# Sums of the quarters of x for block pairs on GpSimd instead of VectorE

## The chip, the cores and the metric

The kernel runs on one core of a Trainium2 chip. The metric is the device time of one execution in microseconds. A core has a matrix engine (TensorE, PE in the profile), a vector engine (VectorE, DVE), an engine for activation functions (ScalarE, ACT), a general engine (GpSimd, POOL) and one that issues DMAs (SyncE, SP). Each works through its own queue in the order in which the kernel has issued its instructions, and waits at an instruction until what it needs from other engines is there.

## The reference

The kernel computes a small decoder of two layers for 256 tokens of width 1024, all in float32. Each layer has four parts, each between two RMS norms:

```python
x += 0.5 * post(SwiGLU_1(pre(x)))     # ffn(l, 0): (silu(x W_gate) * (x W_up)) W_out, width 2816
x += post(Mixer(pre(x)))              # layer 0: mLSTM; layer 1: differential attention
x += 0.5 * post(SwiGLU_2(pre(x)))     # ffn(l, 1)
x += post((p[i] W_ple) * sigmoid(pre(x) W_gate))
```

Between the layers, keys and values are computed once from the normed x. Nearly all the time goes into products of x (256 x 1024) with weight matrices that are read from HBM in blocks of 1 MB.

## The kernel before

**Float32 products out of three.** TensorE works on the type fp32r, which holds fewer bits than float32. So each operand is split in two: a high part (ScalarE copies it to fp32r: tiles `xh`, `whi`, `hh`) and the leftover (VectorE subtracts the high part: `xl`, `wlo`, `hl`). `split` does both. A product then takes three matmuls: high x high, low x high, high x low. A weight block of 1 MB is 128x2048 in SBUF (`wraw`), and its leftover is one VectorE operation on 128x2048; a quarter of x is 128x512.

**Block pairs.** The weights of a hidden layer come in blocks of columns, a block for each 256 columns. `block_pair` (from L718) computes two blocks for both halves of the tokens in seven products instead of eight, in the manner of Strassen and Winograd. For that it needs sums of weight blocks and sums of quarters of x. The weights are `w11`, `w21`, `w22` (blocks as they are), `wt3` and `wu1` (a block loaded by SyncE's DMA, with a second block added by an accumulating DMA that GpSimd issues) and `wt2`, `wt4` (VectorE adds two `wraw` tiles). The quarters are made in `forms` (L700 to L712), once for all the pairs of a part: with a11, a12, a21, a22 the quarters of the normed and transposed x (tiles `att`, 128x512 float32),

- s1 = a21 - a22
- s3 = a11 - a21
- s2 = s1 - a11
- n4 = a12 + s2

and each is split into `xh` and `xl`. `forms` is called five times: for ffn(0,0) (place 1), for the mLSTM's input product (place 2), for ffn(0,1) (place 3), ffn(1,0) (place 4) and ffn(1,1) (place 5). At places 3 to 5 its operations are marked urgent, since the pairs begin right behind the norm; at places 1 and 2 they are not. In the profile of the kernel before, the sums lie at 42.5 to 52.3, 213.9 to 226, 303.5 to 308, 514.6 to 518.4 and 797.5 to 803.7 us. All pairs of a part use the first product with w11 and w21 and the unsummed quarters; then s2 with wt2, s1 with wu1, s3 with wt3, n4 with w22.

**What sets the order.** The kernel's code isn't issued as it is written. A recording layer collects all operations with the tiles that they read and write; `cost` (L212 to L257) gives each a duration; `play` (L267 to L428) simulates the engines with these durations and gives every engine the order in which its operations are issued, urgent ones and those of higher rank first; and `issue` (L430) then issues them. So nearly every instruction of the profile has the line L433, and tiles tell them apart. The plan also hands out the buffers, so that a tile such as `wlo_4r` holds one thing in one plan and another thing in the next. `play` lets a GpSimd operation end no earlier than 170 ns after the last VectorE operation with two SBUF inputs; a VectorE operation waits in the plan for no GpSimd operation but those whose result it reads. A duration in `cost` that changes moves operations on every engine.

The other work of GpSimd is small: powers of the norms' means (tiles `sm`, 128x1), masks, and the accumulating DMAs of the pairs.

## Time and profile before

| what | value |
|---|---|
| median of three runs | 1003.71 us (1002.12, 1003.71, 1003.89) |
| the profiled execution's own time | 1002.59 us |
| its span in the trace | 1000.8 us |
| instructions in the trace | 12442 |
| granted TensorE clock | 0.997 |
| data read from HBM | 263.40 MB |
| GpSimd: busy time, instructions | 94.9 us, 126 |

The page gives for each engine the time in which it was busy, and its share of the span. A row of a timeline has the start in us, the duration, the engine, the line, the operation with its tiles (out<-in, buffer numbers of rotating tiles are part of the name where they matter), shapes and types, and the count where a row stands for several of the same kind; in brackets stand the idle time of the engine ahead of it and what ended that. A row of a group has the busy time in us and the mean of one in ns, then idle time. Engines' records overlap a little: a VectorE operation is shown until its result is written, and the next begins some 80 ns earlier.

### The profile page before, as it was taken

How to read it: one execution, taken by the hardware profiler on the slowest of the kernel's cores; microseconds unless marked ns; L12 is line 12 of the kernel's file. 1: busy time of each engine (PE TensorE's matmuls, PEld its weight loads, DVE VectorE, ACT ScalarE, POOL GpSimd, SP SyncE). 2: the span in 40 equal slices, each digit the busy share in tenths (PEclk: the TensorE clock that was granted, in tenths of full speed). 3: DMA queues.
4: the chain of work that ended last, by engine and by line, in shares of the span. 5: the costliest groups of instructions: out<-in, count | busy, mean ns of one | idle time of the engine just before them, and what ended most of it. 6: DMA issues, size and time to landing. Idle time of an engine off the chain costs nothing.

```text
span 1000.8 us, 12442 instructions
## 1 busy us (share of the span) xinstructions
PE 986.4 (99%) x4636; PEld 803.0 (80%) x4636; DVE 892.8 (89%) x909; ACT 698.6 (70%) x924; POOL 94.9 (9%) x126
## 2 busy tenths in 40 slices
PE   9999999999999999999999999999999999999997
PEld 7888888887787778888878888888888887878786
DVE  6977999799999999998799999898984999999983
ACT  7746777578756877685867767686776776757752
POOL 0010000300141000001120000001002300000010
PEclk9999999999999999999999999999999999999998
DMA  9999948765699999765699999864759899996621
GB/s 345 420 339 343 311 179 296 244 207 198 255 320 340 326 309 335 279 247 207 261 301 330 324 353 347 329 244 161 253 210 285 235 297 318 313 295 252 242 84 43
DMA packets 45859, 274.68 MB, mean 274 GB/s; under 512 B 5480, under 2 KB 5864, under 8 KB 16104
## 3 DMA queue, kind: packets, MB, share of 16 engines
q1 hardware_dynamic: 39752, 231.69, 60.2%
q0 software_dynamic: 5760, 41.95, 20.6%
q8 instruction: 36, 0.59, 0.2%
q10 hardware_dynamic: 288, 0.27, 0.1%
q14 instruction: 23, 0.19, 0.1%
HBM read 263.40 MB, written 10.49 MB: 274 GB/s over the span
## 4 chain that ended last, share of the span: by engine, by line
PE 47%; issue 2%; ACT 2%; POOL 1%; DVE 1%; DVEq 0%; POOLq 0%; ACTq 0%
PE accI L433 30%; PE accO L433 15%; PE tr L433 2%; POOL sm L433 1%; ACT sg L433 1%; DVE wlo_4r L433 0%; ACT att L433 0%; DVE wlo_2r L433 0%; ACT wraw L433 0%; ACT whi_5r L433 0%; ACT whi_0r L433 0%; DVE wraw L433 0%; DVE att L433 0%; DVE xl_5r L433 0%; DVEq L1498 0%
## 5 line engine op out<-in xcount | busy, mean ns | idle before, releaser
L433 DVE TENSOR_TENSOR wraw<-wraw,wraw 128x2048 f32<-128x2048 f32 x40 | 91.4, 2284 | 0.1
L433 ACT ACTIVATE whi_1r<-wraw 128x2048 fp32r<-128x2048 f32 (+2 forms) x49 | 72.7, 1494 | 18.2 <-PE accI L433 8.8
L433 ACT ACTIVATE whi_4r<-wraw 128x2048 fp32r<-128x2048 f32 (+1 forms) x45 | 75.4, 1684 | 11.9 <-issue 4.4
L433 ACT ACTIVATE whi_2r<-wraw 128x2048 fp32r<-128x2048 f32 (+1 forms) x48 | 79.4, 1661 | 5.5 <-issue 2.6
L433 ACT ACTIVATE whi_5r<-wraw 128x2048 fp32r<-128x2048 f32 (+1 forms) x47 | 79.2, 1694 | 5.6 <-PE accI L433 4.7
L433 ACT ACTIVATE whi_0r<-wraw 128x2048 fp32r<-128x2048 f32 (+2 forms) x48 | 74.5, 1557 | 6.8 <-PE accI L433 3.4
L433 ACT ACTIVATE whi_3r<-wraw 128x2048 fp32r<-128x2048 f32 (+1 forms) x45 | 73.6, 1647 | 3.3 <-PE accI L433 1.6
L433 ACT ACTIVATE att<-accI 128x512 f32<-128x512 f32 x80 | 47.5, 594 | 38.1 <-PE accI L433 37.8
L433 POOL DMA_DIRECT2D wraw<-in_ffn_in x36 | 32.0, 889 | 343.5 <-DMA wraw<-in_ffn_in 286.3
L433 POOL TENSOR_SCALAR sm<-sm 128x1 f32<-128x1 f32 x32 | 23.5, 735 | 308.8 <-ACT sg L433 308.8
L433 POOL TENSOR_TENSOR sm<-sm,mhalf 128x1 f32<-128x1 f32 (+2 forms) x40 | 30.7, 769 | 108.2 <-DVE sm L433 105.6
L433 ACT ACTIVATE sg<-att,sm 128x256 f32<-128x256 f32 x54 | 26.9, 502 | 16.9 <-DVE att L433 16.8
L433 ACT ACTIVATE sg<-accO 128x512 bf16<-128x512 f32 (+2 forms) x46 | 20.2, 445 | 25.0 <-PE accO L433 21.0
L433 ACT ACTIVATE sg<-accI,sm 128x256 f32<-128x256 f32 x34 | 16.0, 470 | 29.3 <-PE accI L433 27.3
L433 PEld LDWEIGHTS tr<-ident,sg 128*128 128x128 f32 x176 | 23.0, 140 | 14.6 <-DVE hl_2r L433 2.7
L433 PE MATMUL tr<-ident,sg 128*128 128x128 f32 x176 | 34.0, 274 | 0.3 <-DVE hl_2r L433 0.3
L433 DVE SCALAR_TENSOR_TENSOR wraw<-wraw,sm,wraw 128x512 f32<-128x512 f32 x32 | 22.7, 749 | 12.0 <-POOL sm L433 11.9
L433 DVE TENSOR_TENSOR att<-accI,att 128x512 f32<-128x512 f32 x40 | 27.4, 685 | 3.3 <-PE accI L433 2.9
L433 ACT ACTIVATE sg<-wraw 128x512 bf16<-128x512 f32 x32 | 20.1, 630 | 13.7 <-DVE wraw L433 9.7
L433 ACT ACTIVATE att<-accI,sm 128x512 f32<-128x512 f32 (+1 forms) x22 | 14.8, 671 | 20.8 <-PE accI L433 20.8
L433 DVE SCALAR_TENSOR_TENSOR sg<-att,sm,sg 128x256 f32<-128x256 f32 x54 | 25.7, 480 | 1.7 <-ACT sg L433 1.5
L433 DVE TENSOR_TENSOR att<-att,att 128x512 f32<-128x512 f32 (+1 forms) x33 | 22.4, 679 | 3.8 <-ACT att L433 3.6
(610 smaller groups left out, 3249.9 us busy)
## 6 DMA issues: line engine op xcount, KB each, us to landing
wraw<-in_ffn_in SPq DMA_DIRECT2D x102, 1024.0 KB, 9.4
wraw<-in_ffn_out SPq DMA_DIRECT2D x44, 1024.0 KB, 8.3
wraw<-in_ffn_in POOLq DMA_DIRECT2D x36, 1024.0 KB, 13.3
wraw<-in_mlstm_in SPq DMA_DIRECT2D x14, 1024.0 KB, 5.3
wraw<-in_ple_gate SPq DMA_DIRECT2D x8, 1024.0 KB, 5.1
wraw<-in_w_kv SPq DMA_DIRECT2D x8, 1024.0 KB, 4.8
home<-wraw SPq DMA_DIRECT2D x28, 256.0 KB, 5.1
wraw<-home SPq DMA_DIRECT2D x14, 512.0 KB, 5.4
```

The lines of the kernel that those rows point to most:

```text
L433: getattr(getattr(self.nc, eng), name)(*args, **kw)
```

## The change

The four sums in `forms` are issued to GpSimd instead of VectorE, and `cost` has a new rule for GpSimd's `tensor_tensor`: 560 ns for up to 8 elements a partition, 2.2 ns an element above (1126 ns for 512).

```diff
@@ cost, L256
         elif o.eng == "gpsimd":
-            o.dur = 560 if o.name == "tensor_tensor" else 320 + m
+            o.dur = 320 + m if o.name != "tensor_tensor" else 560 if m <= 8 else 2.2 * m
             o.lat = o.dur + 90
@@ forms, L709
         for out, x0, x1, op, q in (
                 (s1, a21, a22, ALU.subtract, q1), (s3, a11, a21, ALU.subtract, q3),
                 (s2, s1, a11, ALU.subtract, q2), (n4, a12, s2, ALU.add, q4)):
-            nc.vector.tensor_tensor(out, x0, x1, op=op)
+            nc.gpsimd.tensor_tensor(out, x0, x1, op=op)
             split(*q, out)
```

The order of all engines is as before up to place 1; from place 2 on the plan is a new one, with the same number of TensorE instructions.

Place 3, VectorE before. The rows begin with the leftovers of the quarters a11 and a22; `att_100`, `att_103`, `att_105` and `att_102` on the left are s1, s3, s2 and n4:

```order
L433 TENSOR_TENSOR xl_4r<-att_103,xh_4r 128x512
L433 TENSOR_TENSOR hl_0r<-tr_97,hh_0r 128x256
L433 TENSOR_TENSOR xl_0r<-att_99,xh_0r 128x512
L433 TENSOR_TENSOR att_100<-att_103,att_99 128x512
L433 TENSOR_TENSOR att_103<-att_105,att_103 128x512
L433 TENSOR_TENSOR att_105<-att_100,att_105 128x512
L433 TENSOR_TENSOR xl_2r<-att_100,xh_2r 128x512
L433 TENSOR_TENSOR xl_3r<-att_103,xh_3r 128x512
L433 TENSOR_TENSOR xl_1r<-att_105,xh_1r 128x512
L433 TENSOR_TENSOR att_102<-att_102,att_105 128x512
L433 TENSOR_TENSOR att_104<-accI_90,att_104 128x512
L433 TENSOR_TENSOR wraw_82<-wraw_82,wraw_85 128x2048
```

Three sums run in a row here, then their three leftovers, then n4; w21's leftover has been computed earlier.

Place 3, VectorE in the changed kernel; `att_98`, `att_105`, `att_103` and `att_100` are now s1, s3, s2 and n4, `wlo_4r` is the leftover of w21 and `wlo_2r` that of wt2:

```order
L433 TENSOR_TENSOR xl_4r<-att_105,xh_4r 128x512
L433 TENSOR_TENSOR xl_0r<-att_99,xh_0r 128x512
L433 TENSOR_TENSOR hl_0r<-tr_97,hh_0r 128x256
L433 TENSOR_TENSOR xl_2r<-att_98,xh_2r 128x512
L433 TENSOR_TENSOR xl_3r<-att_105,xh_3r 128x512
L433 TENSOR_TENSOR xl_1r<-att_103,xh_1r 128x512
L433 TENSOR_TENSOR wlo_4r<-wraw_79,whi_2r 128x2048
L433 TENSOR_TENSOR xl_4r<-att_100,xh_4r 128x512
L433 TENSOR_TENSOR wlo_2r<-wraw_82,whi_3r 128x2048
```

The sums are gone, and w21's leftover stands behind the leftovers of s1, s3 and s2.

Place 3, GpSimd in the changed kernel (`sm` are the norm's powers, the DMAs add a second block for the next pair):

```order
L433 TENSOR_SCALAR sm_0_156<-sm_15_149 128x1
L433 TENSOR_TENSOR sm_4_160<-sm_0_156,mhalf_133 128x1
L433 TENSOR_TENSOR att_98<-att_105,att_99 128x512
L433 TENSOR_TENSOR att_105<-att_103,att_105 128x512
L433 TENSOR_TENSOR att_103<-att_98,att_103 128x512
L433 TENSOR_TENSOR att_100<-att_100,att_103 128x512
L433 DMA wraw_77<-in_ffn_in 128x2048
L433 DMA wraw_83<-in_ffn_in 128x2048
```

Between the norm's power and the two DMAs, which followed it directly, four sums have come.

Place 4, VectorE in the changed kernel; `att_99`, the second `att_103` and `att_101` are s1, s3 and s2, `wlo_3r` is the leftover of the 128x2048 block w11 and `wlo_1r` that of w21, and the copies are of transposed tiles:

```order
L433 COPY wraw_81<-tr_97 128x4x128
L433 TENSOR_TENSOR xl_2r<-att_103,xh_2r 128x512
L433 TENSOR_TENSOR xl_4r<-att_102,xh_4r 128x512
L433 TENSOR_TENSOR xl_3r<-att_99,xh_3r 128x512
...
L433 COPY wraw_81<-tr_97 128x4x128
L433 TENSOR_TENSOR wlo_2r<-wraw_82,whi_5r 128x1024
L433 TENSOR_TENSOR xl_0r<-att_103,xh_0r 128x512
L433 TENSOR_TENSOR wlo_2r<-wraw_82,whi_5r 128x1024
L433 TENSOR_TENSOR wlo_3r<-wraw_83,whi_1r 128x2048
L433 TENSOR_TENSOR xl_5r<-att_101,xh_5r 128x512
L433 COPY wraw_81<-tr_97 128x4x128
```

The leftover of s3 comes behind four weight leftovers and a copy, that of s2 behind two more; before, the four sums stood between two of the copies.

Place 5, VectorE in the changed kernel; `att_98`, the second meaning of `att_105`, and `att_103` are s1, s3 and s2, and `wlo_4r` is the leftover of wt2:

```order
L433 TENSOR_TENSOR xl_6r<-att_105,xh_6r 128x512
L433 TENSOR_TENSOR xl_1r<-att_100,xh_1r 128x512
L433 TENSOR_TENSOR hl_0r<-tr_97,hh_0r 128x256
L433 TENSOR_TENSOR att_102<-accI_90,att_102 128x512
L433 TENSOR_TENSOR xl_5r<-att_98,xh_5r 128x512
L433 SCALAR_TENSOR_TENSOR sg_128<-att_102,sm_6_162,sg_128 128x256
L433 TENSOR_TENSOR xl_3r<-att_105,xh_3r 128x512
L433 TENSOR_TENSOR xl_2r<-att_103,xh_2r 128x512
L433 TENSOR_TENSOR hl_2r<-tr_97,hh_2r 128x256
L433 TENSOR_TENSOR wlo_4r<-wraw_76,whi_1r 128x2048
```

The rows are those of before without the sums; s1 stood ahead of `xl_6r`, the next two among the following leftovers.

## Prediction

> **What bounds the kernel now.** I read the page's busy shares first, then busy time by engine in the five stretches that hold the five places where the sums are computed (columns: from:to, length, then busy us and count for PE, PEld, DVE, ACT, POOL, then PEclk, DMA share, GB/s).

> ```profile
> PE 986.4 (99%) x4636; PEld 803.0 (80%) x4636; DVE 892.8 (89%) x909; ACT 698.6 (70%) x924; POOL 94.9 (9%) x126
> ...
> 40.00:100.00 60.00, 60.00 (x272) 49.43 (x271) 47.66 (x40) 35.09 (x36) 5.39 (x6) 1.00 1.02 354
> 186.00:250.00 64.00, 64.00 (x318) 52.10 (x317) 60.16 (x70) 48.09 (x59) 7.87 (x9) 1.00 0.63 206
> 300.00:360.00 60.00, 58.26 (x259) 45.51 (x258) 59.61 (x56) 45.19 (x52) 6.12 (x8) 1.00 1.00 330
> 490.00:540.00 50.00, 49.70 (x235) 40.44 (x234) 47.68 (x56) 36.30 (x52) 9.65 (x12) 1.00 0.89 292
> 780.00:850.00 70.00, 67.67 (x305) 54.44 (x304) 68.55 (x65) 51.79 (x60) 11.62 (x11) 1.00 0.90 283
> ```

> TensorE sets the time nearly everywhere: it is never idle in 40:100 and 186:250 and idle 0.30 us in 490:540. The page's 89% for VectorE hides two stretches in which VectorE is the bound: 59.61 of 60 us in 300:360, with TensorE idle 1.74, and 68.55 of 70 in 780:850, with TensorE idle 2.33. Two rows show that TensorE's waits there end on VectorE (the bracket is the idle time before the matmul, and what released it):

> ```profile
> 314.15 0.50 PE L433 MATMUL accI<-wlo_4r,xh_2r 128*128 128x512 f32 x1 [0.65 <-DVE wlo_4r L433]
> ...
> 832.76 0.50 PE L433 MATMUL accI<-wlo_2r,xh_5r 128*128 128x512 f32 x1 [1.03 <-DVE wlo_2r L433]
> ```

> So what GpSimd does is free (9% busy) unless it is late; what VectorE loses or gains counts at place 3 (ffn(0,1), 303 us) and place 5 (ffn(1,1), 797 us), with place 4 (ffn(1,0), 514 us) on the edge.

> **What is removed: 20 sums on VectorE.** At place 3 they stand so (DVE):

> ```profile
> 302.57 0.42 DVE L433 TENSOR_TENSOR hl_0r<-tr,hh_0r 128x256 fp32r<-128x256 f32 x1
> 302.90 0.68 DVE L433 TENSOR_TENSOR xl_0r<-att,xh_0r 128x512 fp32r<-128x512 f32 x1
> 303.50 2.14 DVE L433 TENSOR_TENSOR att<-att,att 128x512 f32<-128x512 f32 x3
> 305.60 0.69 DVE L433 TENSOR_TENSOR xl_2r<-att,xh_2r 128x512 fp32r<-128x512 f32 x1
> 306.20 0.68 DVE L433 TENSOR_TENSOR xl_3r<-att,xh_3r 128x512 fp32r<-128x512 f32 x1
> 306.81 0.69 DVE L433 TENSOR_TENSOR xl_1r<-att,xh_1r 128x512 fp32r<-128x512 f32 x1
> 307.41 0.68 DVE L433 TENSOR_TENSOR att<-att,att 128x512 f32<-128x512 f32 x1
> ```

> Each lasts 0.68 us, but the next starts 0.60 us after it (306.81 to 307.41): four sums are worth 4 x 0.60 = 2.4 us of VectorE per place, 12 us over five.

> **What is added: 20 sums on GpSimd.** No row of before has GpSimd adding 128x512. The nearest rows (GpSimd by form: busy, mean ns):

> ```profile
> L433 POOL MEMSET att<- 128x288 f32 x1 | 0.3, 341 | 27.9 <-DVE att L433 27.9
> L433 POOL MEMSET mhalf<- 128x8 f32 x1 | 0.1, 106 | 0.0
> L433 POOL MEMSET ident<- 128x128 f32 x1 | 0.2, 206 | 0.3 <-POOLq L1496 0.3
> L433 POOL TENSOR_SCALAR_AFFINE_SELECT ident<-ident 128x128 f32<-128x128 f32 x1 | 0.3, 287 | 0.0
> ```

> Writing costs (341-106)/280 = 0.84 ns an element; an operation that also reads one input costs (287-206)/128 = 0.63 ns more. If writing and two reads add up, a sum is 0.106 + 512 x 0.84 + 2 x 512 x 0.63 = 1.18 us, an estimate; if reads hide behind the write, 0.54; with a read as dear as a write, 1.40. I take 1.18, as the select row is the only one with an input. [...]

> One sum takes twice as long as on VectorE and the three of s1, s3, s2 are a chain on one engine. How the two engines get along is the next question:

> ```profile
> 293.97 4.20 POOL L433 TENSOR_SCALAR sm<-sm 128x1 f32<-128x1 f32 x1 [5.03 <-ACT sg L433]
> ...
> 301.12 0.30 POOL L433 TENSOR_SCALAR sm<-sm 128x1 f32<-128x1 f32 x1 [2.30 <-ACT sg L433]
> 301.51 0.56 POOL L433 TENSOR_TENSOR sm<-sm,mhalf 128x1 f32<-128x1 f32 x1
> ...
> 293.60 2.28 DVE L433 TENSOR_TENSOR wlo_2r<-wraw,whi_5r 128x2048 fp32r<-128x2048 f32 x1
> 295.80 2.28 DVE L433 TENSOR_TENSOR wlo_4r<-wraw,whi_2r 128x2048 fp32r<-128x2048 f32 x1
> ```

> The operation that takes 0.30 us at 301.12 takes 4.20 us at 293.97: it ends at 298.17, just behind two VectorE operations back to back (to 298.08) that read two SBUF tiles each. So a GpSimd operation waits for such VectorE operations, and doesn't get between two of them. Every leftover (xl, wlo) and every wraw sum is of that kind. Whether a long GpSimd operation holds VectorE in turn, no row shows.

> [...]

> **Places 1 and 2: 0.** Both are computed ahead of need; VectorE is busy 47.66 of 60 and 60.16 of 64 us there, and TensorE 60.00 of 60 and 64.00 of 64. If GpSimd held VectorE for all of 4 x 1.18, VectorE would lose 4.7 - 2.4 = 2.3 us, within 12.34 and 3.84 us of slack.

> **Place 3: +1.2 (0 to +1.9).** In the new order VectorE runs the leftovers xl_4r, xl_0r, hl_0r, then those of s1, s3 and s2, and only then w21's wlo_4r, which before stood ahead of the sums (295.80); it has changed places with a wraw sum (308.61 before) of the same 2.28 us, so the work behind is as much as it was. s1 can start beside hl_0r, which reads one SBUF tile; xl_4r, xl_0r before it end at 301.96 + 0.69 + 0.60 = 303.25. Without any holding: three sums, 303.25 + 3 x 1.18 = 306.8; ACT's high part, 0.62; the leftover of s2, 0.68: w21's turn at 308.1. Before, this point of the queue was reached at 308.01 (behind n4, which VectorE no longer computes): 0. With holding: s1 to 304.4, s3 to 305.6, leftover of s1 to 306.3, s2 to 307.5, leftover of s3 to 308.2, then either the leftover of s2 (w21 at 308.9) or n4 first (310.0): +0.8 to +1.9. ACT's part and the rows behind:

> ```profile
> 305.98 0.63 ACT L433 ACTIVATE xh_1r<-att 128x512 fp32r<-128x512 f32 x1
> ...
> 308.01 0.68 DVE L433 TENSOR_TENSOR att<-accI,att 128x512 f32<-128x512 f32 x1
> 319.47 2.28 DVE L433 TENSOR_TENSOR wlo_1r<-wraw,whi_4r 128x2048 fp32r<-128x2048 f32 x1
> 321.67 2.28 DVE L433 TENSOR_TENSOR wraw<-wraw,wraw 128x2048 f32<-128x2048 f32 x1
> ...
> 326.19 2.29 DVE L433 TENSOR_TENSOR wraw<-wraw,wraw 128x2048 f32<-128x2048 f32 x1
> ```

> Behind it VectorE runs without a gap until past 321.67, so the loss stays in its queue, and as VectorE is the bound TensorE pays it. I take +1.2, between the held cases and the free one, nearer to the held. The two accumulating DMAs of the next pair now stand behind four sums in GpSimd's queue (before: 302.11 and 304.01):

> ```profile
> 302.11 0.95 POOL L433 DMA_DIRECT2D wraw<-in_ffn_in  x1
> 304.01 0.86 POOL L433 DMA_DIRECT2D wraw<-in_ffn_in  x1 [0.94 <-DVE xl_0r L433]
> ...
> wraw<-in_ffn_in POOLq DMA_DIRECT2D x36, 1024.0 KB, 13.3
> ```

> Issued at about 309.4, the first lands at 322.7 (13.3 us), and its first reader is the wraw sum at 326.19: hidden by 3.5 us; a longer wait in GpSimd's queue than that would show.

> **Place 4: +1.2 (0 to +2.1).** The rows that count:

> ```profile
> 513.96 0.69 DVE L433 COPY wraw<-tr 128x512 f32<-128x512 f32 x1
> ...
> 520.16 0.69 DVE L433 COPY wraw<-tr 128x512 f32<-128x512 f32 x1
> ...
> 529.31 2.28 DVE L433 TENSOR_TENSOR wlo_3r<-wraw,whi_4r 128x2048 fp32r<-128x2048 f32 x1
> ...
> 532.82 0.47 PE L433 MATMUL accI<-wlo_3r,xh_1r 128*128 128x512 f32 x1
> ```

> The wlo_3r (w21) ends at 531.59 and is used at 532.82: 1.23 us of cover. If the engines take turns, s1 runs beside the copy, which reads no second SBUF tile, and three sums hold VectorE: 3 x 1.18 - 2.4 = +1.1, covered: 0. If GpSimd never gets between back-to-back operations, as at 293.97, s3 waits for the copy at 520.16 and s2 for a gap behind the next leftovers; by the order, w21's leftover then ends near 534.9 against 532.8: +2.1. The 4.20 us row is the only one on this question and shows starving, so I take a little more than the middle, +1.2.

> **Place 5: +1.0 (-0.4 to +1.2).**

> ```profile
> 797.46 0.69 DVE L433 TENSOR_TENSOR att<-att,att 128x512 f32<-128x512 f32 x1
> ...
> 804.59 2.28 DVE L433 TENSOR_TENSOR wlo_1r<-wraw,whi_2r 128x2048 fp32r<-128x2048 f32 x1
> ...
> 807.10 0.40 PE L433 MATMUL accI<-wlo_1r,xh_2r 128*128 128x512 f32 x1
> ```

> s1 starts at 797.46 before; in the new order two leftovers go first and s1 gets in beside hl_0r, at 798.8; s3 ends at 801.2, s2 at 803.1 (its turn comes behind the leftover of s1), the leftovers of s3 and s2 bring wt2's leftover to 805.8 to 806.0, against 804.59: +1.2 to +1.4. It ends at 806.87 and is used at 807.10, so 0.23 of it is covered: +1.0 to +1.2. Without holding it would start at 804.2, 0.4 earlier.

> **Sum.** 0 + 0 + 1.2 + 1.2 + 1.0 = +3.4 us; ends -0.4 and +5.2. The profiled execution took 1002.59 us (span 1000.8 and 1.8 around it), 1.1 below the median, 1003.71. On the median: 1003.71 + 3.4 = 1007.1; its own range is 1005 to 1009.

> **Rivals.**
> (A) GpSimd doesn't hold VectorE, and its chains end in time. For it: in before, GpSimd operations are so small that none is seen to delay VectorE. Against: the 4.20 us row shows that the two exclude each other. Sum of the lower ends: 0 + 0 - 0.4 = -0.4, so 1003.3.
> (B) The other side: the 2.4 us that VectorE is relieved of at places 3 and 5 comes through, and TensorE's waits in the stretches that VectorE bounds vanish; decisive is whether leftovers wait for sums or sums for leftovers. The cap is TensorE's idle time there, 1.74 + 2.33 = 4.1: 999.6. For it: 59.61 of 60 us busy. Against: s2's leftover needs three sums in a row, at 1.18 instead of 0.60.
> (C) Each sum holds VectorE for its whole 1.18 us at places 3 to 5: 3 x (4 x 1.18 - 2.4) = +7, and the changed order adds a wait of the size of the largest in before (1.03): 1011.7. For it: VectorE runs two-input operations back to back at all three. Against: part of each sum falls beside copies and PSUM reads.
> That the sums stay on VectorE is excluded: the order of the changed kernel has 20 additions of 128x512 on GpSimd.

> **How the numbers follow.** Forecast 0.45, A 0.25, B 0.15, C 0.15. Two times of this kernel differ by up to 0.18% (1002.12 to 1003.89), so 0.2%, 2 us, is what can be told from no change. Faster: B, and a little of A: 0.17. Same: most of A and the forecast's lower tail: 0.26. Slower: the rest of the forecast and C: 0.57. The range for 8 in 10 leaves out half of B and the tail of C: 1000.0 to 1012.5.

> **What would show it.** The 20 GpSimd rows: near 1.18 us where VectorE leaves gaps, 3 us and more where two-input operations run back to back. VectorE's next leftover should start when a sum ends, not inside it; if leftovers of 0.68 us overlap sums unchanged, rival A's step is right. At place 3 the matmul on w21's low part should wait for VectorE; in 300:360 TensorE's idle time should rise from 1.74 to about 3, in 780:850 from 2.33 to 3.3. Idle time below 1 in both, or a sum above 2 us in a gap of VectorE, would refute the forecast.

## The result, and the profile after

The changed kernel takes 1018.51 us (median of 4 runs, 1016.79 to 1019.40) against 1003.06 us before (median of 4): a ratio of 1.0154, 95% interval 1.0141 to 1.0168. It is slower by 15.5 us; the prediction had +3.4 and a range up to 1012.5.

The page's busy shares and busy time by stretch of the changed kernel (same columns as before; the stretches are later here by what has been lost ahead of them); its profiled execution took 1018.3 us with a span of 1016.4:

```profile
PE 992.6 (98%) x4636; PEld 806.5 (79%) x4636; DVE 898.3 (88%) x889; ACT 700.9 (69%) x924; POOL 128.6 (13%) x146
...
40.00:100.00 60.00, 57.61 (x253) 46.98 (x252) 43.95 (x35) 29.97 (x30) 5.73 (x7) 0.97 1.02 345
186.00:250.00 64.00, 62.16 (x305) 49.12 (x304) 56.98 (x61) 44.60 (x54) 14.19 (x16) 1.00 0.62 193
300.00:360.00 60.00, 56.31 (x242) 43.93 (x242) 57.67 (x47) 41.58 (x49) 15.50 (x12) 0.97 1.00 329
540.00:780.00 240.00, 237.63 (x1167) 194.16 (x1166) 217.19 (x228) 173.40 (x260) 16.21 (x23) 0.99 0.81 278
780.00:850.00 70.00, 68.15 (x326) 54.73 (x325) 59.18 (x62) 48.68 (x70) 19.23 (x19) 1.00 0.89 271
```

VectorE has 20 instructions less and is busy for 5.5 us more (898.3 against 892.8). TensorE, which was never idle in 40:100, is idle for 2.39 us there, and in two rows its granted clock is 0.97. Of these stretches only 780:850 has TensorE less idle than before.

Where the time goes is read best from TensorE's own progress. For the table, all its matmuls are added up by the columns that they stream, and it is noted how much later than in the trace of before the same sum is reached. The columns are points in the time of before: 56 lies behind place 1, place 2 between 205 and 290, place 3 between 290 and 370, place 4 between 500 and 560, place 5 between 790 and 960. The lower rows are runs of the next part. Each row is a single profiled execution: that of place 1 alone is the fastest of its five runs, that of place 2 alone the slowest of its five.

| later than before (us) at | 56 | 205 | 290 | 370 | 500 | 560 | 790 | 960 |
|---|---|---|---|---|---|---|---|---|
| changed kernel | 4.8 | 4.8 | 8.8 | 12.7 | 12.7 | 16.8 | 16.7 | 16.0 |
| new order, sums on VectorE | 1.7 | 1.8 | 5.6 | 6.5 | 6.5 | 8.8 | 8.7 | 7.1 |
| old order, sums on GpSimd | 1.2 | 1.2 | 2.7 | 5.1 | 5.1 | 5.7 | 5.5 | 6.0 |
| place 1 alone on GpSimd | 3.2 | 3.2 | 3.2 | 3.1 | 3.2 | 3.2 | 3.2 | 2.8 |
| place 2 alone | -0.2 | -0.2 | 3.9 | 3.7 | 3.7 | 3.6 | 3.5 | 4.5 |
| places 3 to 5 alone | -0.2 | -0.1 | -0.5 | 2.4 | 2.4 | 6.4 | 6.3 | 5.5 |

The loss comes in steps at places 1 to 4, about 4 us each, and place 5 loses nothing on balance.

At places 1, 3 and 4 a part of the step is a lower clock. In the changed kernel's trace, TensorE's granted clock is 0.50 in three stretches of 3.41 us each (from 46.74, 350.53 and 548.50), each of them behind waits of TensorE. By the ratio of the clocks, as an estimate, work that takes 3.41 us at 0.50 takes 1.7 at 1.00, so the three cost 5.1 us, a third of the loss. Between the first 7 and the last 6 us of the span, the traces of before, of both halves of the change (second and third row) and of place 1 alone have no such stretch; place 2 alone has one (from 835.93) and places 3 to 5 have two (from 312.69 and 537.97).

**What the sums do to VectorE.** Place 1, GpSimd and VectorE in the changed kernel:

```profile
30.21 1.30 POOL L433 TENSOR_TENSOR att<-wraw 128x512 f32<-128x512 f32 x1 [9.32 <-DMA wraw<-in_ffn_out]
31.58 3.21 POOL L433 TENSOR_TENSOR wraw<-wraw 128x512 f32<-128x512 f32 x1
34.87 3.23 POOL L433 TENSOR_TENSOR wraw<-att,wraw 128x512 f32<-128x512 f32 x1
38.18 2.16 POOL L433 TENSOR_TENSOR wraw<-wraw 128x512 f32<-128x512 f32 x1
...
30.37 3.28 DVE L433 TENSOR_TENSOR wlo_0r<-wraw,whi_5r 128x2048 fp32r<-128x2048 f32 x1
33.97 2.98 DVE L433 TENSOR_TENSOR wlo_1r<-wraw,whi_0r 128x2048 fp32r<-128x2048 f32 x1
37.20 4.22 DVE L433 TENSOR_TENSOR wlo_2r<-wraw,whi_1r 128x1024 fp32r<-128x1024 f32 x2
45.75 0.47 DVE L433 SCALAR_TENSOR_TENSOR sg<-accI,sm,sg 128x256 f32<-128x256 f32 x1
```

And VectorE in the same place before:

```profile
30.31 2.28 DVE L433 TENSOR_TENSOR wlo_0r<-wraw,whi_5r 128x2048 fp32r<-128x2048 f32 x1
32.90 2.28 DVE L433 TENSOR_TENSOR wlo_1r<-wraw,whi_0r 128x2048 fp32r<-128x2048 f32 x1
35.43 2.35 DVE L433 TENSOR_TENSOR wlo_2r<-wraw,whi_1r 128x1024 fp32r<-128x1024 f32 x2
42.11 0.48 DVE L433 SCALAR_TENSOR_TENSOR sg<-accI,sm,sg 128x256 f32<-128x256 f32 x1
...
43.16 0.38 PE L433 MATMUL tr<-ident,sg 128*128 128x128 f32 x2
```

A sum alone takes 1.30 us (30.21); the next three take 3.21, 3.23 and 2.16. VectorE's leftovers beside them are each stretched, 2.28 to 3.28, 2.28 to 2.98, 2.35 to 4.22 for two: here the engines take turns, and each waits out the other's operation. The four sums ran as soon as their inputs were there, 12 us ahead of where VectorE computed them (42.50 on), so VectorE had lost 3.6 us when it came to the operation on sg: 45.75 instead of 42.11. Before, its result ended 0.57 us ahead of its transposition by TensorE (42.59 against 43.16). TensorE in the changed kernel:

```profile
46.28 0.44 PE L433 MATMUL tr<-ident,sg 128*128 128x128 f32 x2 [2.39 <-DVE sg L433]
46.47 0.54 PE L433 MATMUL accI<-wlo_0r,xh_1r 128*128 128x512 f32 x1
46.81 0.63 PE L433 MATMUL accI<-whi_5r,xl_1r 128*128 128x512 f32 x1
47.24 0.63 PE L433 MATMUL accI<-whi_0r,xh_3r 128*128 128x512 f32 x1
```

TensorE waits 2.39 us, and behind the wait its matmuls of 128x512 follow one another every 0.43 us instead of every 0.23, until 50.2, the end of the first stretch at half the clock. The VectorE time that the sums used to take later (2.4 us) comes back where TensorE doesn't wait for VectorE, and so buys nothing.

Over the whole kernel VectorE operations are stretched by 16.8 us (all those longer by over 0.12 us than the median of their kind in the trace of before), for 12 us of sums that it no longer does.

### The profile page after: what moved, and what is told of

Read it like the earlier page. It is cut to its first block, busy times and chain, and to the rows that moved or that the text cites. A ratio compares the mean times of both kernels' runs of the same rounds, so it can differ in the third digit from the quotient of the medians.

```text
span 1016.4 us, 12440 instructions
## 1 busy us (share of the span) xinstructions
PE 992.6 (98%) x4636; PEld 806.5 (79%) x4636; DVE 898.3 (88%) x889; ACT 700.9 (69%) x924; POOL 128.6 (13%) x146
## 4 chain that ended last, share of the span: by engine, by line
PE 81%; DVE 10%; ACT 3%; issue 2%; DMA 2%; POOL 1%; SPq 0%; DVEq 0%; POOLq 0%; ACTq 0%
PE accI L433 50%; PE accO L433 28%; PE tr L433 3%; DVE wraw L433 2%; DVE wlo_3r L433 1%; DVE att L433 1%; DVE wlo_4r L433 1%; ACT sg L433 1%; DVE wlo_1r L433 1%; DMA wraw<-in_x 1%; DVE wlo_2r L433 1%; DVE wlo_0r L433 1%; POOL sm L433 1%; DMA wraw<-in_ffn_in 1%; DMA wraw<-in_xT 1%
## 5 line engine op out<-in xcount | busy, mean ns | idle before, releaser
L433 DVE TENSOR_TENSOR wraw<-wraw,wraw 128x2048 f32<-128x2048 f32 x40 | 91.4, 2285 | 0.2
L433 ACT ACTIVATE whi_0r<-wraw 128x2048 fp32r<-128x2048 f32 (+2 forms) x49 | 77.9, 1598 | 10.2 <-DVE wraw L433 7.9
L433 ACT ACTIVATE whi_1r<-wraw 128x2048 fp32r<-128x2048 f32 (+2 forms) x51 | 78.0, 1541 | 9.8 <-PE accO L433 3.9
L433 ACT ACTIVATE whi_5r<-wraw 128x2048 fp32r<-128x2048 f32 (+1 forms) x44 | 71.6, 1639 | 17.7 <-PE accI L433 12.2
L433 ACT ACTIVATE whi_2r<-wraw 128x2048 fp32r<-128x2048 f32 (+1 forms) x46 | 77.6, 1690 | 8.4 <-issue 3.4
L433 ACT ACTIVATE whi_4r<-wraw 128x2048 fp32r<-128x2048 f32 (+1 forms) x48 | 77.5, 1627 | 2.6 <-PE accO L433 1.9
L433 ACT ACTIVATE whi_3r<-wraw 128x2048 fp32r<-128x2048 f32 (+1 forms) x44 | 72.2, 1641 | 9.2 <-PE accI L433 4.1
L433 POOL DMA_DIRECT2D wraw<-in_ffn_in x36 | 32.1, 899 | 306.8 <-DMA wraw<-in_ffn_in 262.9
L433 ACT ACTIVATE att<-accI 128x512 f32<-128x512 f32 x80 | 47.5, 594 | 29.9 <-PE accI L433 29.4
L433 POOL TENSOR_SCALAR sm<-sm 128x1 f32<-128x1 f32 x32 | 20.8, 650 | 308.6 <-ACT sg L433 308.6
L433 POOL TENSOR_TENSOR sm<-sm,mhalf 128x1 f32<-128x1 f32 (+2 forms) x40 | 33.0, 825 | 107.4 <-DVE sm L433 104.8
L433 ACT ACTIVATE sg<-att,sm 128x256 f32<-128x256 f32 x54 | 27.2, 504 | 21.9 <-DVE att L433 21.5
L433 ACT ACTIVATE sg<-accO 128x512 bf16<-128x512 f32 (+2 forms) x46 | 20.2, 444 | 26.0 <-PE accO L433 22.3
L433 PEld LDWEIGHTS tr<-ident,sg 128*128 128x128 f32 x176 | 22.9, 141 | 18.8 <-DVE sg L433 5.2
L433 PE MATMUL tr<-ident,sg 128*128 128x128 f32 x176 | 34.6, 278 | 3.4 <-DVE sg L433 3.3
L433 ACT ACTIVATE sg<-accI,sm 128x256 f32<-128x256 f32 x34 | 16.0, 472 | 31.5 <-PE accI L433 25.6
L433 DVE SCALAR_TENSOR_TENSOR wraw<-wraw,sm,wraw 128x512 f32<-128x512 f32 x32 | 22.7, 749 | 11.1 <-POOL sm L433 11.1
L433 DVE TENSOR_TENSOR att<-accI,att 128x512 f32<-128x512 f32 x40 | 27.4, 686 | 2.8 <-PE accI L433 2.4
L433 DVE SCALAR_TENSOR_TENSOR sg<-att,sm,sg 128x256 f32<-128x256 f32 x54 | 27.0, 501 | 2.8 <-ACT sg L433 2.4
L433 ACT ACTIVATE sg<-wraw 128x512 bf16<-128x512 f32 x32 | 20.1, 629 | 13.2 <-DVE wraw L433 9.1
L433 ACT ACTIVATE att<-accI,sm 128x512 f32<-128x512 f32 (+1 forms) x22 | 14.7, 669 | 20.7 <-PE accI L433 20.7
L433 DVE TENSOR_TENSOR wlo_4r<-wraw,whi_1r 128x2048 fp32r<-128x2048 f32 (+1 forms) x13 | 25.4, 1957 | 1.4 <-PE accI L433 0.7
## 6 DMA issues: line engine op xcount, KB each, us to landing
wraw<-in_ffn_in SPq DMA_DIRECT2D x102, 1024.0 KB, 8.0
wraw<-in_ffn_out SPq DMA_DIRECT2D x44, 1024.0 KB, 8.2
wraw<-in_ffn_in POOLq DMA_DIRECT2D x36, 1024.0 KB, 13.3
wraw<-in_mlstm_in SPq DMA_DIRECT2D x14, 1024.0 KB, 5.2
wraw<-in_ple_gate SPq DMA_DIRECT2D x8, 1024.0 KB, 7.2
wraw<-in_w_kv SPq DMA_DIRECT2D x8, 1024.0 KB, 4.8
```

The source lines that it names most:

```text
L433: getattr(getattr(self.nc, eng), name)(*args, **kw)
```

## The experiments

The theories: **H**, that a sum on GpSimd and a VectorE operation exclude each other in both directions, and VectorE loses more in this way, and earlier, than it saves. **R**, that the new order of all engines costs the time. **L**, that only the sums' own length matters, for those who wait for them.

**The two halves of the change.** First the engine alone: the plan is made as if VectorE computed the sums, and GpSimd gets them.

```diff
-            nc.vector.tensor_tensor(out, x0, x1, op=op)
+            (nc.vector if nc.plan is None else nc.gpsimd).tensor_tensor(out, x0, x1, op=op)
```

> The 20 sums run on GpSimd, but every engine keeps the order that it had before the change (the plan is made as if VectorE computed them). Theory H (a sum on GpSimd and a VectorE operation exclude each other in both directions; each sum stretches a VectorE operation by 0.7 to 1.1 us, as the trace of the changed kernel shows, while VectorE saves 0.60): at least half of the 15.5 us stays, 1010 to 1020 us, and VectorE operations beside the sums last up to 1.1 us longer. Theory R (the new order of the engines costs the time, not the engine): 1003 to 1006 us.

Measured: 1008.90 us, ratio 1.0059 (1.0042 to 1.0076), less than theory H expected and more than R. The stretch of VectorE is 14.1 us against 16.8, and it falls otherwise: in the old order s2 and n4 of place 1 stand behind GpSimd's accumulating DMA at 49.65, so that only two sums come early, and place 1 costs 1.2 us instead of 4.8. At place 2 the old order loses 1.5 us, though almost nothing is stretched there (0.3 us): a sum waits out VectorE's 128x2048 leftover and takes 3.71 us, ScalarE waits for GpSimd, and TensorE for a high part of ScalarE's (`xh_3r`):

```profile
218.54 3.71 POOL L433 TENSOR_TENSOR att<-wraw 128x512 f32<-128x512 f32 x1
...
223.72 0.60 ACT L433 ACTIVATE att<-accI 128x512 f32<-128x512 f32 x1 [1.90 <-POOL att L433]
...
225.41 0.50 PE L433 MATMUL accI<-whi_5r,xh_3r 128*128 128x512 f32 x1 [1.44 <-ACT xh_3r L433]
```

Then the order alone: the changed kernel's plan, and the sums issued to VectorE.

```diff
-            nc.gpsimd.tensor_tensor(out, x0, x1, op=op)
+            (nc.gpsimd if nc.plan is None else nc.vector).tensor_tensor(out, x0, x1, op=op)
```

> The other half: all engines keep the order of the changed kernel, but the 20 sums are issued to VectorE at their place in it. Theory H: no VectorE operation is stretched, and the time falls back to 1001 to 1007 us (an order made for another engine may cost a few us). Theory R: 1014 to 1020 us.

Measured: 1010.29 us, ratio 1.0073 (1.0053 to 1.0092): also between the two. No VectorE operation is stretched. So each of the two theories accounts for a part of the loss: 0.59% and 0.73% add up to 1.32% of 1.54%. The rest is within the intervals; a part may be the changed kernel's three stretches at half the clock, which neither of these two traces has. By the table the order's part is 1.7 us at place 1, where VectorE now does two of the sums ahead of its operation on sg, 3.8 in the mLSTM behind place 2, 0.9 at place 3 and 2.3 at place 4, and it gives 1.6 back at the end. Three of TensorE's longer waits in this run (two for VectorE, one for ScalarE):

```profile
277.68 0.73 PE L433 MATMUL accO<-wlo_0r,xh_0r 128*128 128x512 f32 x2 [1.08 <-DVE wlo_0r L433]
...
343.88 0.50 PE L433 MATMUL accI<-whi_1r,xh_1r 128*128 128x512 f32 x1 [1.17 <-ACT whi_1r L433]
...
540.12 0.50 PE L433 MATMUL accI<-wlo_1r,xh_1r 128*128 128x512 f32 x1 [0.75 <-DVE wlo_1r L433]
```

**The hold by itself.** The kernel before, with four additions on GpSimd put beside VectorE's leftovers at 30 us, on a tile (`scr`) that the kernel does not use until long after; the sums stay on VectorE. `n` counts VectorE's operations of 128x2048, so that `n == 0` is the leftover at 30.3 us; the addition of one column makes the others wait for that leftover's input `whi`.

```diff
+        scr = self.made[f"sb:att:{F32}", 7][:, :512]
+        self.nc.gpsimd.memset(scr, 0.0)
...
+                if n == 0:
+                    whi = args[2]
+                    self.nc.gpsimd.tensor_tensor(scr[:, :1], whi[:, :1], whi[:, :1], op=ALU.add)
+                    for _ in range(4):
+                        self.nc.gpsimd.tensor_tensor(scr, scr, scr, op=ALU.add)
```

> The kernel before with its order, plus four additions of 128x512 on GpSimd from the moment at which VectorE starts the leftover at 30.3 us; nobody reads what they write. Theory H: VectorE operations between 30 and 42 us are stretched by 3 to 4.5 us in all, the VectorE operation on sg that stood at 42.1 us comes near 45.7, TensorE waits about 2.5 us for it as in the changed kernel and runs at a lower rate behind the wait: 1007 to 1009 us. Rival L (only the length of the chain of sums counts, 1.3 us each for 0.6): nobody waits for these, so 1002 to 1004 us and no stretched VectorE operation.

> As the run with four added additions, but with ten GpSimd memsets of 128x512 in their place (about 5 us of GpSimd, which write SBUF and read nothing). Theory H, if what excludes the two engines is the reading: no VectorE operation is stretched by more than 0.2 us, 1002 to 1004 us. If any GpSimd operation of this length holds VectorE: as with the additions, 1007 to 1009 us.

Measured: 1006.11 us with the additions, ratio 1.0026 (1.0016 to 1.0036); 1001.98 us with memsets, ratio 0.9993 (0.9984 to 1.0002). GpSimd, VectorE and TensorE with the additions:

```profile
29.60 9.12 POOL L441 TENSOR_TENSOR att<-att 128x512 f32<-128x512 f32 x4
...
29.72 3.07 DVE L443 TENSOR_TENSOR wlo_0r<-wraw,whi_5r 128x2048 fp32r<-128x2048 f32 x1
33.11 2.73 DVE L443 TENSOR_TENSOR wlo_1r<-wraw,whi_0r 128x2048 fp32r<-128x2048 f32 x1
36.09 3.70 DVE L443 TENSOR_TENSOR wlo_2r<-wraw,whi_1r 128x1024 fp32r<-128x1024 f32 x2
...
44.65 0.44 PE L443 MATMUL tr<-ident,sg 128*128 128x128 f32 x2 [1.65 <-DVE sg L443]
```

And with the memsets:

```profile
29.75 5.78 POOL L441 MEMSET att<- 128x512 f32 x10
...
29.89 2.28 DVE L443 TENSOR_TENSOR wlo_0r<-wraw,whi_5r 128x2048 fp32r<-128x2048 f32 x1
32.48 2.29 DVE L443 TENSOR_TENSOR wlo_1r<-wraw,whi_0r 128x2048 fp32r<-128x2048 f32 x1
35.02 2.35 DVE L443 TENSOR_TENSOR wlo_2r<-wraw,whi_1r 128x1024 fp32r<-128x1024 f32 x2
```

Nobody reads what these GpSimd operations write, and nothing was moved, so rival L doesn't explain this loss; at place 2 of the old order, where TensorE waits for a sum's high part, it has its share. Writing alone doesn't hold VectorE here: ten memsets, 5.78 us of GpSimd, leave VectorE's 2.28, 2.29 and 2.35 alone. The additions stretch it by 2.6 us, less than the 3 to 4.5 expected; TensorE waits 1.65 us and is 1.6 later at 56 us. By the ratio the kernel loses 2.6 us (1.6 to 3.6), also less than expected. The trace is of the fastest of the eight runs, and loses 1.7 us more in a stretch at half the clock, from 834.00 on.

With the additions the hold goes in both directions: 9.12 us for four additions that take 1.30 each alone, and 3.07 us for a leftover of 2.28.

**Place by place.** `forms` counts its calls, and only those named are given to GpSimd (and planned so).

```diff
+        nc.place = getattr(nc, "place", 0) + 1
+        adder = nc.gpsimd if nc.place in (1,) else nc.vector
...
-            nc.gpsimd.tensor_tensor(out, x0, x1, op=op)
+            adder.tensor_tensor(out, x0, x1, op=op)
```

> Only the four sums of place 1, ffn(0,0), are on GpSimd; the order of everything else stays as before but for a few rows about 30 to 52 us. Theory H: VectorE is held from 30 to 41 us for 3.5 us in all, its operation on sg comes 3.6 us late, TensorE waits 2.4 us for it and runs at half rate for some 3 us behind that; nothing gives it back: 1006 to 1009 us, about +4.5. Theory that place 1 is computed ahead of need and so costs nothing (the prediction's step): 1002 to 1004 us.

> The changed kernel with the sums of place 1 back on VectorE; places 2 to 5 and their new order stay. Theory H with costs that add up: 4 to 5 us below the changed kernel, 1013 to 1015 us. If the places' costs don't add up (later stretches absorb what place 1 loses): 1017 to 1019 us.

Measured: place 1 alone 1006.75 us, ratio 1.0035 (1.0022 to 1.0048); the changed kernel without place 1 1013.44 us, ratio 1.0104 (1.0089 to 1.0119), 5.1 us below the changed kernel. The order of these two runs differs in some 30 rows from that of before and of the changed kernel, so this is the hold almost alone, 3.5 to 5 us, and it adds to the rest. TensorE with place 1 alone:

```profile
46.30 0.44 PE L433 MATMUL tr<-ident,sg 128*128 128x128 f32 x2 [2.41 <-DVE sg L433]
46.50 0.48 PE L433 MATMUL accI<-wlo_0r,xh_1r 128*128 128x512 f32 x1
46.81 0.39 PE L433 MATMUL accI<-whi_5r,xl_1r 128*128 128x512 f32 x1
47.04 0.39 PE L433 MATMUL accI<-whi_0r,xh_3r 128*128 128x512 f32 x1
```

The wait is the same as in the changed kernel (2.41 and 2.39 us), but the matmuls behind it run at 0.23 us. The half rate that was expected here came only in the other trace; it makes 3.2 us into 4.8. Two further runs of place 1 alone, 1007.58 and 1008.21 us, have a mean granted clock of 0.994 against 0.999 in the profiled one, so the half rate may have come in them; they have no trace.

> Only the mLSTM's four sums on GpSimd, with a new order from there on. If the hold there (3 us of VectorE, small operations of the gates among them) costs what the changed kernel falls back between 215 and 290 us of its span: about +4 by then; what the new order costs later is unknown, 0 to +5: 1006 to 1012 us. By the prediction's step (place 2 is computed ahead of need, 0): 1002 to 1004 us.

> Places 1 and 2 on VectorE, places 3, 4 and 5 on GpSimd, with the change's price in the plan; the order is as before up to place 3. From the changed kernel, which falls back by 7.2 us from 285 us of its span on: about 1010 us. By the prediction's sum for these places: 1006.4 us. If VectorE's relief comes through at these places: below 1003 us.

Measured: place 2 alone 1005.43 us, ratio 1.0034 (1.0021 to 1.0047), below what was expected; places 3 to 5 alone 1008.15 us, ratio 1.0061 (1.0046 to 1.0076). Place 2 loses 4.1 us of TensorE's progress between 205 and 290, as the changed kernel does (4.0), but so does the run with the new order and the sums on VectorE (3.8). In the new order, then, this loss is the order's and not the hold's, while in the old order the sums on GpSimd cost 1.5 there. At places 3 to 5 the relief of VectorE doesn't come through on balance; of the trace's 5.5 us, 3.4 are its two stretches at half the clock.

**A new order by itself.** Three kernels with all sums on VectorE, each with another plan: sums planned 60 ns longer, 120 ns shorter, and the plan's constant MARGIN at 350 instead of 300.

```diff
-            o.dur = m / 0.96 / (2 if one else 1) + 70 + (60 if o.name == "scalar_tensor_tensor" else 0)
+            o.dur = m / 0.96 / (2 if one else 1) + 70 + (60 if o.name == "scalar_tensor_tensor" else 0) + 60 * self.summing
```

> No sum moves to GpSimd; the plan alone takes the 20 VectorE sums as 60 ns longer than before, which gives new orders from place 2 on, as the change does. Theory N (the old order is a good one among many, and any new order made by the same rules costs several us): 1005 to 1011 us. Theory G (it is GpSimd's long sums in the plan that make the order of the changed kernel bad): 1001 to 1004 us.

> A second new order without any sum on GpSimd: the plan takes the 20 VectorE sums as 120 ns shorter than before. Theory N (any new order by these rules costs some us against the one before): 1004 to 1010 us, no VectorE operation stretched. Theory that only a longer sum in the plan costs: 1001 to 1004 us.

> A third new order, which touches no duration at all: the constant MARGIN of the plan (how much earlier than its turn a transposition's input must be there) is 350 instead of 300. Theory N: 1004 to 1010 us. If the order before is one of many as good: 1001 to 1004 us.

Measured: 1007.76 us, ratio 1.0050 (1.0033 to 1.0067); 1004.61 us, ratio 1.0021 (1.0010 to 1.0031); 1006.87 us, ratio 1.0042 (1.0028 to 1.0057). None has a stretched VectorE operation, and none is as good as the kernel before: these three new orders cost 2 to 5 us, though no sum has moved. In each trace 1.7 us of that is one stretch at half the clock (from 355.39, 341.50 and 837.21). Why the old order is better than the others tried is not shown. In the first, the loss is made at two waits for ScalarE (2.17 and 1.47 us of idle TensorE) in the ffn behind place 3, the second with the stretch at half the clock behind it (`summing` in the diff is set around the four sums):

```profile
338.68 0.47 PE L433 MATMUL accI<-whi_2r,xh_2r 128*128 128x512 f32 x1 [2.17 <-ACT whi_5r L433]
...
353.98 0.49 PE L433 MATMUL accI<-whi_2r,xh_5r 128*128 128x512 f32 x1 [1.47 <-ACT whi_2r L433]
```

**A plan that knows the hold.** The changed kernel, with a plan in which a sum starts behind the VectorE operation that runs, and a VectorE operation with two SBUF inputs behind the sum that runs.

```diff
-        lock_until = 0.0
+        lock_until = pool_until = 0.0
...
-                if e == "gpsimd" and lock_until > s:
+                if e == "gpsimd" and o.dur > 1000:
+                    end = max(s, lock_until) + o.dur
+                    pool_until = end
+                elif e == "gpsimd" and lock_until > s:
                     end = max(end, lock_until + 170)
                 if e == "vector" and o.two:
+                    end = max(end, pool_until + o.dur) if s < pool_until else end
                     lock_until = end
```

> The changed kernel, with a plan that knows the hold: a sum starts behind the VectorE operation with two SBUF inputs that runs, and such a VectorE operation starts behind the sum that runs. If the loss comes from an order that is wrong about the hold: 1005 to 1010 us. If it is the held VectorE time itself (some 13 us of it, wherever the sums are put) and a new order as such: 1012 to 1019 us.

Measured: 1010.97 us, ratio 1.0080 (1.0065 to 1.0095): 7.5 us better than the changed kernel, 7.6 worse than before, between the two expectations. VectorE is stretched as much as ever (17.3 us); at place 1 two sums now stand behind a DMA and nothing is lost by 205 us. Its trace has no stretch at half the clock between its ends; the three of the changed kernel are worth 5.1 of the 7.5 us. So a plan can put the hold where it costs less, but no run here gains by sums on GpSimd.

## Why the prediction was wrong

- **The bound** was read rightly: TensorE sets the time, and the losses begin at TensorE's waits, most of them for VectorE. That the waits in 780:850 end on VectorE was half right: of the 2.33 us idle there, the longest wait, 1.06 us, ended on ScalarE, so rival B's cap took in a wait for ScalarE, and the largest wait of that stretch was this one and not rival C's 1.03:

```profile
831.23 0.50 PE L433 MATMUL accI<-whi_0r,xh_2r 128*128 128x512 f32 x1 [1.06 <-ACT whi_0r L433]
```

- **The price of a sum on GpSimd**, 1.18 us as an estimate, measured 1.30 alone (30.21), and 1.61 in the mean of the twelve between two `att` tiles, waits for VectorE included:

```profile
L433 POOL TENSOR_TENSOR att<-att,att 128x512 f32<-128x512 f32 x12 | 19.3, 1606 | 6.0 <-PE tr L433 4.7 <-DVE xl_2r L433 0.7
```

- **That GpSimd holds VectorE in turn** was left open and taken at half to two thirds. It is so at every place (20 VectorE operations are stretched by 0.15 to 1.4 us each); rival A is refuted. That GpSimd never gets between back-to-back operations is wrong for sums: they take turns (the second sum of place 1 takes 3.21 us, and the leftover beside its end 2.98 instead of 2.28).
- **"Places 1 and 2: 0" is the step that failed first.** The 12.34 us of slack at place 1 were VectorE's idle time summed over a stretch of 60 us. The operation that TensorE was waiting for had 0.57 us of slack, and the sums ran 12 us earlier than the prediction had them, ahead of that operation. Place 1 costs 3.5 us alone and some 5 in the changed kernel. Place 2 isn't 0 either. In the new order it loses 4 us by 290, and nearly as much (3.8) with the sums on VectorE, so that belongs to the next point; in the old order the sums on GpSimd alone cost 1.5, by a wait for a sum's high part.
- **A term was missing: the price of a new order.** The sum followed the new order at five places and took it as equal to the old one elsewhere. The order alone costs 7.3 us in this change, and 2 to 5 in three others.
- **A second term was missing: a wait of TensorE cost more than its own length.** Three stretches at half the clock, 1.7 us each, follow waits in the changed kernel, 5.1 of the 15.5 us. The trace of before shows none between its first 6 and its last 5 us, so the forecast had no row to take it from; where they fall is in part chance (last section; the five runs of place 1 alone have mean granted clocks from 0.994 to 0.999).
- **Place 3: +1.2 (0 to +1.9).** w21's leftover was forecast for 308.9 to 310.0 in the time of before. It starts at 317.93, and xl_4r, the start of the chain, at 310.53 instead of 301.96, 8.57 later: 309.36, as forecast, and TensorE waits for it as forecast (the forecast's +0.8 to +1.9 are counted from its own 308.1; from the 308.01 of before they are 0.1 more):

```profile
310.67 6.79 POOL L433 TENSOR_TENSOR att<-att,att 128x512 f32<-128x512 f32 x4
...
317.93 2.28 DVE L433 TENSOR_TENSOR wlo_4r<-wraw,whi_2r 128x2048 fp32r<-128x2048 f32 x1
...
320.27 0.50 PE L433 MATMUL accI<-wlo_4r,xh_6r 128*128 128x512 f32 x1 [1.45 <-DVE wlo_4r L433]
```

  The place as a whole lost 3.9 us up to 370 in the time of before. Of that, 0.9 are the order's and 1.7 the second stretch at half the clock (350.53 to 353.94), behind two waits of 1.17 and 0.69 us that the order alone has too. The 1.3 us left are near the forecast.
- **Place 4: +1.2 (0 to +2.1).** The wait came true at the upper end, though by another way: VectorE is stretched by 3.9 us instead of sums being starved, and w21's leftover ends 2.3 us too late.

```profile
526.79 1.28 POOL L433 TENSOR_TENSOR att<-att,att 128x512 f32<-128x512 f32 x1 [4.71 <-PE tr L433]
528.77 5.55 POOL L433 TENSOR_TENSOR att<-att,att 128x512 f32<-128x512 f32 x3 [0.70 <-DVE xl_2r L433]
...
547.87 0.50 PE L433 MATMUL accI<-wlo_1r,xh_1r 128*128 128x512 f32 x1 [2.30 <-DVE wlo_1r L433]
```

  The run with the order alone already loses 2.3 us there and waits 0.75; with the hold 4.1, of which 1.7 are the third stretch at half the clock (548.50 to 551.92). In the old order the hold costs 0.6, near the lower end.
- **Place 5: +1.0.** The table's two upper rows differ by 0.9 us from 790 on (8.0 at 790, 8.9 at 960): right in size, but not by the step that was forecast. TensorE doesn't wait for wt2's leftover; its waits there are for hl_0r (0.29) and sg (0.69):

```profile
825.31 0.39 PE L433 MATMUL accI<-wlo_4r,xh_2r 128*128 128x512 f32 x1
```

  The new order gives 1.6 back there, so that the changed kernel gains 0.7, and TensorE's idle time in 780:850 falls from 2.33 to 1.85 where 3.3 was forecast.
- **Rival C** (each sum holds VectorE for its whole length, 1011.7) was nearest in mechanism: 16.8 us for 20 sums are 0.84 us a sum, and up to 1.4 for one VectorE operation.
- Which rows of the new order make the 3.8 us in the mLSTM is open; that it is the order follows from its being nearly the same on either engine.

## What to carry to other kernels

Slack is a property of the operation that the bounding engine waits for, not of a stretch: before work is put on another engine, follow the first late operation on the queue that it shares or holds up. Two engines that exclude each other, as a sum and a leftover did here (1.30 us alone to 3.21, 2.28 to 3.28), are one engine for the time that they share; moving an operation of 0.60 us to a neighbour that needs 1.3 for it makes the pair slower, and earlier, if the neighbour starts as soon as its inputs are there. And where a plan sets the order, a changed cost is a change to every engine: measure the new order with the old engine, and some neutral new orders, before the engine is blamed or praised. Where a trace shows the granted clock fall behind waits, count that apart: of two nearly equal waits here, 2.39 and 2.41 us, it followed the first and not the second.

## What the runs showed that was not expected

```profile
43.33:46.74 3.41, 1.02 (x6) 0.60 (x5) 3.41 (x4) 0.00 (x0) 0.00 (x0) 1.00 1.01 418
46.74:50.16 3.42, 3.42 (x9) 2.64 (x9) 3.22 (x4) 2.81 (x3) 0.74 (x1) 0.50 1.02 424
...
42.10:45.51 3.41, 1.79 (x8) 1.13 (x7) 3.41 (x2) 0.35 (x1) 0.00 (x0) 1.00 1.02 423
45.51:48.92 3.41, 2.62 (x13) 2.20 (x14) 3.41 (x6) 2.01 (x2) 0.00 (x0) 1.00 1.02 423
```

  In the changed kernel the three steps of the grid ahead of the stretches at half the clock have 2.39, 1.85 and 2.30 us of idle TensorE, and between the span's first and last 6 us no other step has over 1.34; with place 1 alone, the step with 1.62 was not followed by one. Two short waits were followed by one where they fell into the same step: the two of about 1.0 us at 830 us lie in two steps in the trace of before (1.22 and 0.88 us of idle time), which keeps its clock, and in one step in the run with four additions, which loses it at 834.00. The grid falls otherwise on the same waits from trace to trace; by what rule the clock follows them is not shown.
- **Not every held operation had two large inputs.** At place 2, VectorE's copy of 4x256 takes 1.28 us beside the sums (before, 0.28), and an operation of 4x256 behind it 1.78 (before, 0.41):

```profile
221.32 1.28 DVE L433 COPY att<-att 4x256 f32<-4x256 f32 x1
...
223.19 1.78 DVE L433 SCALAR_TENSOR_TENSOR att<-att 4x256 f32<-4x256 f32 x1
```

  while copies from PSUM beside sums (0.69 us at 219.30 and at 526.68) are not stretched.
